# Reordering the first splits of a decoder layer, and placing two gate units between the memory's key units

## The chip, the cores and the metric

The kernel runs on one core of one Trainium2 chip. The metric is the device time of one execution in microseconds (us). Before the change it is 808.86 us, the median of three runs (808.32 to 809.01).

The engines are named as the profile does: PE is TensorE, whose sequence of matmuls is followed here, and PEld its weight loads; ACT is ScalarE, DVE VectorE, POOL GpSimd, and SP SyncE, which issues most transfers.

## The reference, cut to what matters

One layer of a decoder over 512 tokens of width 1024, in float32. The normalised input `u` is projected by one wide matrix, and its columns feed three branches: sliding-window attention, stick-breaking attention and cross-attention to a memory of 256 rows. Each branch's output is projected back, multiplied by the sigmoid of its own gate columns, and the three are added. An output projection and a gated feed-forward network follow.

```python
u = rms_norm(h, ln_mix_pre[l])
proj = jnp.einsum('bsd,de->bse', u, w_in[l])
qa, ka, va, qb, kb, vb, qm, gl = jnp.split(proj, split_idx, axis=-1)
y_swa = swa_sink_attention(qa, ka, va, swa_sinks[l], rel_bias)
y_sb = stick_breaking_attention(qb, kb, vb)
mkv = jnp.einsum('bmd,de->bme', rms_norm(mem, ln_mem[l]), w_mem_kv[l])
mk, mv = jnp.split(mkv, 2, axis=-1)
y_mem = memory_cross_attention(qm, mk, mv)
g = jax.nn.sigmoid(gl.reshape(B, S, N_BRANCH, D))
...
```

(The reshapes to heads are left out of the calls.)

## The kernel before, in words

**Numbers.** Every float32 operand of the large products is split into a high part of the fp32r type (a copy on ScalarE) and a low part (value minus high part, on VectorE); see `split`, L132 to L139. A product is then three matmuls, high by high, high by low and low by high (`mm3`, L164 to L168). In the profile a row `hi<-raw` is the first half of a split, `lo<-raw,hi` the second.

**The stream of weight units.** `Stream` (L33) holds a list of units: each has a weight block of 128 x 1024 numbers (512 KB), loaded through SP, split into hi and lo, and then used by a generator that issues matmuls. When a unit begins, loads up to four units ahead and splits up to three units ahead are put out (`ahead`, L58; constants L28 and L29). A unit's generator yields after each small group of matmuls the time that the group is taken to cost: 0.65 for three matmuls of 512 columns, 0.325 for three of 256. A projection or gate unit (`proj`, L278; `gate`, L306) has eight groups of 0.65; a unit of the memory's keys (`mem_keys`, L374) eight groups of 0.325; a unit of its values (`mem_vals`, L389) four groups of 0.65.

**Who asks for units.** The attention code runs beside the stream. `sb_head` (L620) does one head of the stick-breaking branch: a first group of score matmuls into three banks `z`, then on ScalarE and VectorE a chain (Abs, Exp, Ln, maximum, splits sh and sl), `yield 7.0`, a second group of matmuls into `z` (sums of the chain's results), three Exp on ScalarE, and `yield 3.0`. After every second head, a product with the values (`ysb`) follows. At each yield the loop at L802 lets the stream put out units worth that time (`dn.run`). So eight heads take 80 of the stream's time, and whatever units come next lie between the heads.

**Order on the engines.** The program's order is only a wish: a planner orders the instructions of each engine at build time, by program order where it holds an instruction for ready. At the start (`with tc.manual_schedule()`, L506 to L555) the order is as written.

**Banks.** The accumulators of projections, gates, keys and values come from a pool of two PSUM banks (`psd`, L110), those of heads from a pool of six (`psa`). A unit's bank is free again when VectorE has evacuated it: L290 for projections and gates, L383 for keys, L401 for values. A key unit uses one bank; the four value units together accumulate into both.

**The order of units** (L435 to L467): four `kb`, four `qb`, six units of values of the tokens, `ka`, `qa0`, `qa1`, four key units, four value units, `qa2`, `qa3`, the eight gates of the stick-breaking branch, and so on. The memory is loaded when `ka` is loaded (`mem_load`) and split when `qa1` is split (`mem_split`).

**The start.** Before the stream runs, the first three units (`kb0` to `kb2`) are loaded in three pieces: chunks 0 and 1 of the eight along the inner dimension (128 x 256 numbers), then 2 to 4, then 5 to 7 (`first_load`, L497; `PIECE`, L492). x is loaded transposed, in eight chunks of 128 x 512. `first_split` (L502) splits one unit's piece; `gain_split` (L485) multiplies one chunk of x by its gain and splits it (`gained`, L235: L237 on ScalarE gives `uh`, L238 on VectorE gives `ul`). TensorE begins with ten warm-up matmuls on an idle tile, then takes nine matmuls for chunk 0 of the three units in an order written out by hand (L543 to L546), and then, chunk by chunk, unit by unit (L547 to L550). Behind the third unit's last chunk comes the sum of squares `ss_x` from `xacc` (L534 to L538).

Of the kernel before, what the change touches and what calls it, by code (L numbers as in the profile page):

```python
# [17 lines left out]
P = 128  # L18
# [3 lines left out]
KC = D // P  # L22
# [4 lines left out]
SWA, SB, MEM = 0, 1, 2  # L27
# [76 lines left out]
def tile_kernel(ctx, tc, a):  # L104
# [13 lines left out]
    def ck(name, dt=F32):  # L118
        return ckp.tile([P, 512], dt, tag="ck", name=name)
# [42 lines left out]
    dn = Stream(w_load, w_split)  # L162

    def mm3(out, l, r, start, stop):  # L164
        (lh, ll), (rh, rl) = l, r
        nc.tensor.matmul(out, lh, rh, start=start, stop=False, skip_group_check=True)  # L166
        nc.tensor.matmul(out, lh, rl, start=False, stop=False, skip_group_check=True)  # L167
        nc.tensor.matmul(out, ll, rh, start=False, stop=stop, skip_group_check=True)  # L168

    def mm(out, l, r, start, stop):  # L170
        return nc.tensor.matmul(out, l, r, start=start, stop=stop, skip_group_check=True)  # L171

    def cols(hl, o, n):
        return hl[0][:, o : o + n], hl[1][:, o : o + n]
# [68 lines left out]
    u = [None] * KC  # L243

    def parts(name, t):
        h, l = ck(f"{name}h", F32R), ck(f"{name}l", F32R)
        split(t[:, :], h[:, :], l[:, :])
        return h, l

    def stack_parts(kind, idx, t):  # L250

        for e in range(2):
            r, o = 64 * e, 64 - 64 * e
            x = ck(f"{kind}s{idx}{e}", F32R)
            nc.scalar.copy(x[r : r + 64, :], t[r : r + 64, :])
            nc.vector.tensor_tensor(
                x[o : o + 64, :], t[r : r + 64, :], x[r : r + 64, :].bitcast(F32), op=ALU.subtract
            )
            st[(kind + "s", idx, e)] = x

    def stack_twice(kind, idx, t):

        for e in range(2):
            r, o = 64 * e, 64 - 64 * e
            x = ck(f"{kind}s{idx}{e}", F32R)
            lo = ck(f"{kind}l{idx}{e}", F32R)
            nc.gpsimd.memset(lo[o : o + 64, :].bitcast(F32), 0.0)
            st[(kind + "l", idx, e)] = lo
            nc.scalar.copy(x[r : r + 64, :], t[r : r + 64, :])
            nc.vector.tensor_tensor(  # L270
                lo[r : r + 64, :], t[r : r + 64, :], x[r : r + 64, :].bitcast(F32), op=ALU.subtract
            )
            nc.vector.tensor_copy(x[o : o + 64, :], t[r : r + 64, :])
            st[(kind + "s", idx, e)] = x

    first_ps = {}

    def proj(kind, idx):  # L278
        def gen(hi, lo):
            begun = first_ps.get((kind, idx))  # L280
            ps = begun or (aps if kind == "kb" or (kind, idx) == ("qb", 2) else dps)(f"{kind}{idx}")
            for k in range(1 if begun else 0, KC):
                mm3(ps[:, :], cols((hi, lo), k * P, P), u[k], k == 0, k == KC - 1)
                yield 0.65
            t = ck(f"{kind}{idx}")
            s = 0.125 if kind in ("qa", "qb") else 1.0

            def evac():
                with tc.high_priority():
                    nc.vector.scalar_tensor_tensor(t[:, :], ps[:, :], s, st["rb"][:, :], op0=ALU.mult, op1=ALU.mult)  # L290
                if kind in ("kb", "qa"):
                    stack_parts(kind, idx, t)
                elif kind in ("qb", "ka"):
                    stack_twice(kind, idx, t)
                elif kind == "qm":
                    st[("qms", idx)] = parts(f"qms{idx}", t)

            if "rb" in st:
                evac()
            else:  # L300
                st.setdefault("waiting", []).append(evac)
            st[(kind, idx)] = t

        return gen
# [69 lines left out]
    def mem_keys(i):  # L374
        def gen(hi, lo):
            if i % 2 == 0:
                st[("mk", i // 2)] = ck(f"mk{i}")
            t = st[("mk", i // 2)][:, (i % 2) * M : (i % 2 + 1) * M]
            ps = dps(f"pmk{i}")
            for k in range(KC):  # L380
                mm3(ps[:, :M], cols((hi, lo), k * P, P), mu[k], k == 0, k == KC - 1)
                yield 0.325
            nc.vector.tensor_tensor(t, ps[:, :M], st["mrb"][:, :], op=ALU.mult)  # L383
            if i % 2 == 1:
                st[("mks", i // 2)] = parts(f"mks{i // 2}", st[("mk", i // 2)])

        return gen
# [49 lines left out]
    for h in range(2):  # L437
        for q in range(3):
            n = 3 if q < 2 else 2
# [3 lines left out]
    def add_proj(kind, idx, ci):  # L443
        src = a["w_p"][:, ci].rearrange("p k n -> p (k n)")
        dn.add(src, 1024, gate(int(kind[1]), idx) if kind[0] == "g" else proj(kind, idx))
# [1 line left out]
    add_proj("ka", 0, 16)  # L447
    dn.on_load(mem_load)
    add_proj("qa", 0, 12)
    add_proj("qa", 1, 13)  # L450
    dn.on_split(mem_split)
    for i in range(4):
        dn.add(a["w_mk"][:, i].rearrange("p k n -> p (k n)"), 1024, mem_keys(i))
    for q in range(4):
        dn.add(a["w_mv"][:, 2 * q : 2 * q + 2].rearrange("p k n -> p (k n)"), 1024, mem_vals(q))
    add_proj("qa", 2, 14)
    add_proj("qa", 3, 15)
    for b, order in ((SB, 0), (SWA, 1), (MEM, 2)):
        for c in range(8):
            add_proj(f"g{b}", c, 17 + 3 * c + b)  # L460
        dn.mark(f"gates{b}")
        if b == SB:
            for i in range(4):
                add_proj("qm", i, 8 + i)
        for c2 in range(4):
            dn.add(a["w_br"][:, b, 2 * c2 : 2 * c2 + 2].rearrange("p c k n -> p (c k n)"), 1024, branch(b, c2, order))
        dn.mark(f"branch{b}")  # L467
# [17 lines left out]
    def gain_split(k):  # L485
        h, l = ck(f"uh{k}", F32R), ck(f"ul{k}", F32R)
        gained(xraw[k][:, :], g_pre[:, k : k + 1], h[:, :], l[:, :])
        u[k] = (h[:, :], l[:, :])


    FIRST = 3
    PIECE = ((0, 2), (2, 5), (5, 8))  # L492
    raws = [wp.tile([P, 1024], F32, tag="raw", name=f"raw_first{i}") for i in range(FIRST)]
    his = [wp.tile([P, 1024], F32R, tag="hi", name=f"hi_first{i}", bufs=4) for i in range(FIRST)]
    los = [wp.tile([P, 1024], F32R, tag="lo", name=f"lo_first{i}", bufs=4) for i in range(FIRST)]
# [6 lines left out]
    def first_split(i, p):  # L502
        sl = slice(PIECE[p][0] * P, PIECE[p][1] * P)
        split(raws[i][:, sl], his[i][:, sl], los[i][:, sl])

    with tc.manual_schedule():  # L506

        idle = cst.tile([P, 512], BF16, name="idle")
        nc.vector.memset(idle[:, :], 0.0)
        pw = dps("warm")  # L510
        for i in range(WARM):
            mm(pw[:, :], idle[:, :P], idle[:, :], True, True)

        first_load(nc.scalar, 0)
        first_table = nc.scalar.preload_act_table_set("natural_log_exp_and_others")
        load_x(0, 3)
        first_load(nc.sync, 1)
        load_x(3, 5)
        first_load(nc.sync, 2)
        load_x(5, 8)  # L520
        dn.loaded = dn.have = FIRST
        first_split(0, 0)
        gain_split(0)
        for i in range(1, FIRST):
            first_split(i, 0)
        gain_split(1)
        gain_split(2)
        for p in (1, 2):
            for i in range(FIRST):
                first_split(i, p)  # L530
            for k in range(*PIECE[p]):
                if u[k] is None:
                    gain_split(k)
        xacc = ck("xacc")  # L534
        nc.scalar.activation(xacc[:, :], xraw[0][:, :], AF.Square)
        for k in range(1, KC):
            nc.scalar.activation(xraw[k][:, :], xraw[k][:, :], AF.Square)
            nc.vector.tensor_tensor(xacc[:, :], xacc[:, :], xraw[k][:, :], op=ALU.add)  # L538
        dn.ahead(4, 3)

        for i in range(FIRST):
            first_ps[("kb", i)] = aps(f"kb{i}")
        for n, (i, w, r) in enumerate(  # L543
            ((0, his, 0), (0, los, 0), (1, his, 0), (0, his, 1), (1, his, 1), (1, los, 0), (2, his, 0), (2, his, 1), (2, los, 0))
        ):
            mm(first_ps[("kb", i)][:, :], w[i][:, :P], u[0][r], n in (0, 2, 6), False)  # L546
        gens = [dn.units[i]["mm"](his[i], los[i]) for i in range(FIRST)]  # L547
        for k in range(1, KC + 1):
            for g in gens:
                next(g, None)  # L550
        dn.at = FIRST
        st["rs"], st["rb"] = rstd_of("x", xacc, S, aps)
        st["chain"] = since[-1]
        for f in st.pop("waiting"):
            f()  # L555
# [864 lines left out]
```

## Time and profile before

| what | value |
|---|---|
| median of three runs | 808.86 us |
| lowest, highest | 808.32, 809.01 us |
| the profiled execution's own time | 808.77 us |
| its span, first to last instruction | 807.0 us |
| granted TensorE clock, mean | 0.998 |

Rows of the profile name the line, engine and operation, then `output<-inputs`, partitions and elements. In a timeline the first two numbers are the start and the duration in us, and brackets at the end give the idle time of the engine before that row and what ended it. In the list of waits the numbers are the sum, the count and the longest in us. The row of a stretch gives its length, the busy time and count of PE, PEld, DVE, ACT and POOL, the granted clock, the share of the DMA engines and GB/s. Matmul rows overlap one another, so that the distance between starts tells the pace and not the duration.

### The profile page before, as it was taken

To read this page: it belongs to the slowest core of one execution; us is meant where nothing else is said; L and a number is where in the kernel's file an instruction comes from. 1 tells how busy PE (TensorE), PEld (TensorE's weight loads), DVE (VectorE), ACT (ScalarE), POOL (GpSimd) and SP (SyncE) were. 2 spreads that over 40 slices of the span, in tenths; PEclk is the share of its full clock that TensorE was granted. 3 is DMA by queue.
4 is the path that set the end of the run, shared out by engine and by line. 5 is a ranking of instruction groups with operands and counts; after the bars stand their busy time and mean duration, and the time that the engine had idled before them with its cause. 6 is when DMAs were issued, how large, how long until landed. Compare 5 with 4: busy or idle time off the path is not lost.

```text
span 807.0 us, 12317 instructions
## 1 busy us (share of the span) xinstructions
PE 797.5 (99%) x4710; PEld 701.1 (87%) x4710; DVE 587.3 (73%) x937; ACT 439.7 (54%) x787; POOL 88.7 (11%) x108
## 2 busy tenths in 40 slices
PE   9999999999999999999999999999999999999996
PEld 6899897778788888888888899999999999988885
DVE  7895878556588833873394869877676777898797
ACT  7562776555655432552272567654444445666573
POOL 1203200000000000320004200010000000205200
PEclk9999999999999999999999999999999999999999
DMA  7444526112222223213359936977777662759902
GB/s 270 140 122 137 189 79 183 53 52 69 63 79 58 90 88 89 69 53 105 97 167 377 234 65 172 264 200 203 186 175 192 174 170 82 180 129 224 211 0 105
DMA packets 37692, 112.95 MB, mean 140 GB/s; under 512 B 4480, under 2 KB 6192, under 8 KB 37632
## 3 DMA queue, kind: packets, MB, share of 16 engines
q1 hardware_dynamic: 29184, 86.32, 33.5%
q0 software_dynamic: 8016, 25.44, 16.7%
q8 instruction: 37, 0.61, 0.3%
q10 hardware_dynamic: 432, 0.39, 0.1%
q14 instruction: 23, 0.19, 0.1%
HBM read 108.46 MB, written 3.67 MB: 139 GB/s over the span
## 4 chain that ended last, share of the span: by engine, by line
PE 96%; DVE 1%; ACT 1%; DMA 1%; issue 1%; ACTq 0%; DVEq 0%
PE g L166 5%; PE g L168 5%; PE g L167 5%; PE gx L166 5%; PE gx L168 5%; PE gx L167 5%; PE z L171 3%; PE br L166 3%; PE br L167 3%; PE br L168 3%; PE gy L168 3%; PE gy L166 3%; PE gy L167 3%; PE x L166 2%; PE x L168 2%; PE x L167 2%
## 5 line engine op out<-in xcount | busy, mean ns | idle before, releaser
L134 ACT CAST hi<-gw 128x1024 fp32r<-128x1024 f32 x77 | 79.7, 1048 | 82.6 <-DVE gw L1005 39.2
L134 ACT CAST hi<-raw 128x1024 fp32r<-128x1024 f32 (+2 forms) x64 | 65.8, 1035 | 101.3 <-issue 49.4
L135 DVE TENSOR_TENSOR lo<-gw,hi 128x1024 fp32r<-128x1024 f32 x77 | 93.4, 1222 | 32.4 <-ACT hi L134 32.4
L135 DVE TENSOR_TENSOR lo<-raw,hi 128x1024 fp32r<-128x1024 f32 (+2 forms) x64 | 78.0, 1219 | 14.8 <-ACT hi L134 14.7
L166 PE MATMUL g<-uh,hi 128*128 128x512 f32 x192 | 75.6, 394 | 0.0
L168 PE MATMUL g<-uh,lo 128*128 128x512 f32 x192 | 74.8, 389 | 0.0
L167 PE MATMUL g<-ul,hi 128*128 128x512 f32 x192 | 74.8, 389 | 0.0
L290 DVE SCALAR_TENSOR_TENSOR g<-g,rb_x 128x512 f32<-128x512 f32 x24 | 16.4, 689 | 54.6 <-PE g L168 54.5
L987 POOL DMA_DIRECT2D gw<-in_w_gu x27 | 23.4, 905 | 187.9 <-DMA gw<-in_w_gu 83.3
L166 PEld LDWEIGHTS g<-uh,hi 128*128 128x128 f32 x192 | 36.1, 188 | 8.1 <-issue 1.0
L168 PEld LDWEIGHTS g<-uh,lo 128*128 128x128 f32 x192 | 36.0, 188 | 7.6
L167 PEld LDWEIGHTS g<-ul,hi 128*128 128x128 f32 x192 | 36.1, 188 | 7.2
L167 PE MATMUL x<-lo,lh 128*128 128x512 f32 x88 | 34.3, 389 | 0.0
L166 PE MATMUL x<-hi,lh 128*128 128x512 f32 x88 | 34.3, 389 | 0.0
L134 ACT CAST hi<-r 128x1024 fp32r<-128x1024 f32 (+1 forms) x24 | 23.6, 982 | 19.6 <-PE y L168 5.3
L168 PE MATMUL x<-hi,ll 128*128 128x512 f32 x88 | 34.1, 389 | 0.0
L135 DVE TENSOR_TENSOR lo<-r,hi 128x1024 fp32r<-128x1024 f32 (+1 forms) x24 | 27.1, 1129 | 3.2 <-ACT hi L134 3.1
L184 ACT ACTIVATE e<-e 128x384 f32<-128x384 f32 (+1 forms) x48 | 26.9, 561 | 1.5
L135 DVE TENSOR_TENSOR lo<-bp,hi 128x512 fp32r<-128x512 f32 x33 | 22.8, 724 | 6.1 <-ACT hi L134 6.0
L134 ACT CAST hi<-bp 128x512 fp32r<-128x512 f32 x33 | 19.1, 620 | 13.6 <-PE y L168 4.8
L654 DVE SCALAR_TENSOR_TENSOR e<-z,e 128x384 f32<-128x384 f32 (+1 forms) x24 | 14.3, 596 | 15.7 <-ACT e L184 15.7
L166 PE MATMUL gx<-B11h,hi 128*128 128x256 f32 x88 | 25.1, 285 | 0.2 <-ACT B11h L916 0.2
(548 smaller groups left out, 2614.3 us busy)
## 6 DMA issues: line engine op xcount, KB each, us to landing
gw<-in_w_gu SPq DMA_DIRECT2D x57, 512.0 KB, 5.3
raw<-in_w_p SPq DMA_DIRECT2D x38, 512.0 KB, 3.6
gw<-in_w_gu POOLq DMA_DIRECT2D x27, 512.0 KB, 7.6
raw<-in_w_br SPq DMA_DIRECT2D x12, 512.0 KB, 3.8
bp<-in_w_dn SPq DMA_DIRECT2D x22, 256.0 KB, 8.2
r<-in_w_dn POOLq DMA_DIRECT2D x10, 512.0 KB, 8.5
raw<-in_w_out SPq DMA_DIRECT2D x8, 512.0 KB, 3.8
bp<-in_w_dn POOLq DMA_DIRECT2D x11, 256.0 KB, 13.2
```

Of the source, the lines that this page charges most:

```text
L134: ins = nc.scalar.copy(hi, raw)
L135: lows = nc.vector.tensor_tensor(lo, raw, hi.bitcast(F32), op=ALU.subtract)
L166: nc.tensor.matmul(out, lh, rh, start=start, stop=False, skip_group_check=True)
L167: nc.tensor.matmul(out, lh, rl, start=False, stop=False, skip_group_check=True)
L168: nc.tensor.matmul(out, ll, rh, start=False, stop=stop, skip_group_check=True)
L171: return nc.tensor.matmul(out, l, r, start=start, stop=stop, skip_group_check=True)
L184: ins = nc.scalar.activation(*args, **kw)
L290: nc.vector.scalar_tensor_tensor(t[:, :], ps[:, :], s, st["rb"][:, :], op0=ALU.mult, op1=ALU.mult)
L654: nc.vector.scalar_tensor_tensor(x, z[i][:, :n], 0.0, x, op0=ALU.max, op1=ALU.add)
L987: nc.gpsimd.dma_start(gw[(n, key)][:, :], g_src(n, i, j), accum_op=ALU.add)
```

## The change

At the start, a piece of a unit and a chunk of x alternate on ScalarE and VectorE: unit 0, chunk 0, unit 1, chunk 1, unit 2, chunk 2, where before it was unit 0, chunk 0, units 1 and 2, chunks 1 and 2. TensorE takes chunk 0 of units 0 and 1 in the order that it had, then chunk 1 of units 0 and 1, then chunks 0 and 1 of unit 2. The stream's generators of these three units go on with chunk 2.

In the stream, `qa1` moves behind the value units, beside `qa2` and `qa3`. Gate 0 of the stick-breaking branch comes between the second and third key units, and gate 1 between the fourth and the value units. The memory is split when the first key unit is split, which is the unit at the same place of the list as `qa1` was. The list stays as long as it was.

```diff
-            for k in range(1 if begun else 0, KC):
+            for k in range(2 if begun else 0, KC):
...
-    add_proj("qa", 1, 13)
-    dn.on_split(mem_split)
+
     for i in range(4):
         dn.add(a["w_mk"][:, i].rearrange("p k n -> p (k n)"), 1024, mem_keys(i))
+        if i == 0:
+            dn.on_split(mem_split)
+        if i % 2 == 1:
+            add_proj(f"g{SB}", i // 2, 17 + 3 * (i // 2) + SB)
     for q in range(4):
         dn.add(a["w_mv"][:, 2 * q : 2 * q + 2].rearrange("p k n -> p (k n)"), 1024, mem_vals(q))
-    add_proj("qa", 2, 14)
-    add_proj("qa", 3, 15)
+    for i in range(1, 4):
+        add_proj("qa", i, 12 + i)
     for b, order in ((SB, 0), (SWA, 1), (MEM, 2)):
-        for c in range(8):
+        for c in range(2 if b == SB else 0, 8):
...
-        first_split(0, 0)
-        gain_split(0)
-        for i in range(1, FIRST):
+        for i in range(FIRST):
             first_split(i, 0)
-        gain_split(1)
-        gain_split(2)
+            gain_split(i)
...
-        for n, (i, w, r) in enumerate(
-            ((0, his, 0), (0, los, 0), (1, his, 0), (0, his, 1), (1, his, 1), (1, los, 0), (2, his, 0), (2, his, 1), (2, los, 0))
-        ):
-            mm(first_ps[("kb", i)][:, :], w[i][:, :P], u[0][r], n in (0, 2, 6), False)
+        order = [(0, 0, "hh"), (0, 0, "lh"), (1, 0, "hh"), (0, 0, "hl"), (1, 0, "hl"), (1, 0, "lh")]
+        order += [(i, k, x) for i, k in ((0, 1), (1, 1), (2, 0), (2, 1)) for x in ("hh", "lh", "hl")]
+        for i, k, x in order:
+            w = (his if x[0] == "h" else los)[i]
+            mm(first_ps[("kb", i)][:, :], w[:, k * P : (k + 1) * P], u[k][x[1] == "l"], k == 0 and x == "hh", False)
         gens = [dn.units[i]["mm"](his[i], los[i]) for i in range(FIRST)]
-        for k in range(1, KC + 1):
+        for k in range(2, KC + 1):
```

## The prediction

> **What bounds the kernel now.** I read the page first, then what TensorE waited for, then the stretches, then the rows around each wait. From the page:
>
> ```profile
> PE 797.5 (99%) x4710; PEld 701.1 (87%) x4710; DVE 587.3 (73%) x937; ACT 439.7 (54%) x787; POOL 88.7 (11%) x108
> ```
>
> TensorE is busy 99% of the span. The change adds and removes no matmul, so it can give back only what TensorE loses between matmuls, and it can lose any amount. The view of the waits of TensorE lists what it lost to other engines. It has five rows; of these, two lie where the diff doesn't reach (the warm-up before any data, and a later stage), and three are in the two places that it edits:
>
> ```profile
> PE ysb L171 <- ACT e L184: 1.1, 1, 1.1
> PE kb L167 <- DVE ul L238: 0.2, 1, 0.2
> PE pmv L166 <- DVE mk L383: 0.2, 1, 0.2
> ```
>
> They are 1.5 us in sum. The stretch that holds two of them:
>
> ```profile
> 120.00:140.00 20.00, 18.71 (x97) 15.77 (x97) 17.12 (x25) 13.80 (x24) 0.00 (x0) 1.00 0.59 173
> ```
>
> TensorE was busy for 18.71 of 20.00 us: 1.29 idle, which are the ysb wait and the pmv wait. The granted clock was 1.00.
>
> **Part 1, the start.** The timeline of TensorE:
>
> ```profile
> 6.31 0.62 PE L171 MATMUL kb<-ul,hi_first 128*128 128x512 f32 x2
> 6.77 0.40 PE L171 MATMUL kb<-uh,lo_first 128*128 128x512 f32 x1
> ...
> 8.48 0.50 PE L167 MATMUL kb<-ul,hi_first 128*128 128x512 f32 x1 [0.22 <-DVE ul L238]
> 8.82 0.40 PE L168 MATMUL kb<-uh,lo_first 128*128 128x512 f32 x1
> 9.06 0.40 PE L166 MATMUL kb<-uh,hi_first 128*128 128x512 f32 x1
> ```
>
> Unhindered, one start follows another after 0.23 to 0.24 us (two from 6.31 to 6.77, one from 8.82 to 9.06). The rows at 6.77 and 8.82 are the sixth matmul of the list written out by hand and the third behind its nine: six steps, which need 6 x 0.235 = 1.41 and took 2.05. So **0.64 us** is lost, three times what the waits list names, because restarts after a wait count as busy. What was late, on ScalarE and then on VectorE:
>
> ```profile
> 5.12 0.41 ACT L134 CAST hi_first<-raw_first 128x256 fp32r<-128x256 f32 x1
> 6.60 0.41 ACT L134 CAST hi_first<-raw_first 128x256 fp32r<-128x256 f32 x1 [1.08 <-DMA raw_first<-in_w_p]
> 6.92 1.33 ACT L237 ACTIVATE uh<-xT,xg 128x512 fp32r<-128x512 f32 x2
> ```
>
> ```profile
> 5.88 0.42 DVE L135 TENSOR_TENSOR lo_first<-raw_first,hi_first 128x256 fp32r<-128x256 f32 x1
> ...
> 7.67 1.41 DVE L238 SCALAR_TENSOR_TENSOR ul<-xT,xg,uh 128x512 fp32r<-128x512 f32 x2 [0.20 <-ACT uh L237]
> ```
>
> ScalarE stands 1.08 us until the third unit's weights land, with chunk 1 of x queued behind them. The view of tile xT, for its first transfer alone:
>
> ```profile
> L482 SPq DMA_DIRECT2D xT<-in_xT x1: 421/421/421, 1.2 to 1.2; - x1
> ...
> DMA to landing us min/median/max: 3.7/3.7/3.7
> ```
>
> Chunk 1 is there at 1.2 + 3.7 = 4.9. With the new order its gain split (half of 1.33, 0.7) begins on ScalarE near 5.12 + 0.41 = 5.5, inside the idle time, and ends by 6.2. VectorE is free at 6.30 and has the low half by 7.05 (half of 1.41 is 0.7). The new order of matmuls asks for that chunk at 6.77 + 0.23 = 7.00 and for its low half two starts later, 7.47: both are there. The third unit's weights, cast from 6.60 to 7.01, are asked for after six more starts, near 8.4. So no wait is left, and I take the whole 0.64. The casts after it move up by one gain split, about 0.6, so they aren't later than now. Nothing is issued anew: the loads and their queues stay as they are. The next thing that could hold TensorE is the sum of squares:
>
> ```profile
> 19.47 1.49 DVE L538 TENSOR_TENSOR xacc<-xacc,xT 128x512 f32<-128x512 f32 x2
> ```
>
> It ends at 20.96. TensorE's row that needs it:
>
> ```profile
> 22.71 1.02 PE L171 MATMUL ss_x<-xacc,ones 128*128 128x512 f32 x2
> ```
>
> 22.71 - 0.64 = 22.07 is still 1.1 us later than 20.96, so the gain isn't given back there.
>
> The Trainium skill, "TensorE: Matmul & The Clock Gate", section "Back-to-back issue gap", gives a warm gap of N/2.4 + 2.5 ns, 216 ns at 512 columns. By it the six steps would need 1.30 and the gain would be 0.75 and the sum 806.9, an estimate; the rows show 0.23 to 0.24, and they decide.
>
> **Part 2, the memory stage.** No instruction is added; units trade places, each with its load and its split. The loads:
>
> ```profile
> raw<-in_w_p SPq DMA_DIRECT2D x38, 512.0 KB, 3.6
> ```
>
> They are asked for four units ahead and land in 3.6 us. By the costs in the code four key or value units last 4 x 2.6 = 10.4, and with gates between them longer, so I cost the loads at nothing; they would cost what a load is late if that cover went. The splits keep their number and, with a gate between the keys, get more time on ScalarE and VectorE. In the stream's own costs a projection or gate is 8 x 0.65 = 5.2, a key or value unit 2.6. Before, ka, qa0, qa1 (15.6), four key units and four value units (20.8) end at 36.4. Each head takes 7.0 and 3.0, so head 3's second group of score matmuls (z) is put out at 37, when the next unit is qa2. It needs a psd bank, and the value units hold both until they are evacuated (L401). The timelines of TensorE and ScalarE and the view of tile pmv:
>
> ```profile
> 134.65 0.39 PE L171 MATMUL z<-sh,ntri_r 128*128 128x512 f32 x1
> ...
> 136.63 0.38 PE L171 MATMUL z<-e,none 128*128 128x128 f32 x2
> 138.12 0.44 PE L171 MATMUL ysb<-e,v_all 128*64 128x128 f32 x4 [1.11 <-ACT e L184]
> 138.49 0.50 PE L166 MATMUL qa<-uh,hi 128*128 128x512 f32 x1
> ```
>
> ```profile
> 136.71 1.36 ACT L184 ACTIVATE e<-z 128x512 f32<-128x512 f32 x3 [0.81 <-PE z L171]
> ```
>
> ```profile
> L401 DVE TENSOR_SCALAR mv<-pmv,rs_m x2: 742/744/745, 135.3 to 139.2; 128x512 f32<-128x512 f32 x2
> ```
>
> So ysb stands ahead of qa2 on TensorE, which waits 1.11 us for three Exp. After the change the sum is 5.2 x 2 + 2.6 x 2 + 5.2 + 2.6 x 2 + 5.2 = 31.2 before the first value unit: at 37 the stream is in the third, with 41.6 - 37 = 4.6 of matmuls left whose banks are already theirs. The 3.0 between z and ysb can then stand where they stand in the program, and cover 1.36 of Exp. I take **1.11** away.
>
> The 0.18 wait of pmv I leave in the sum. Its rows, TensorE then VectorE:
>
> ```profile
> 123.67 0.47 PE L166 MATMUL pmv<-hi,mh 128*128 128x512 f32 x1 [0.18 <-DVE mk L383]
> ```
>
> ```profile
> 123.11 0.74 DVE L383 TENSOR_TENSOR mk<-pmk,rb_m 128x256 f32<-128x256 f32 x2
> ```
>
> The unit after the keys needs a bank that VectorE frees late. That unit becomes a gate, and the same wait can meet it: between 0.2 gained and the losses of the first rival below.
>
> The sum: 808.77 of the profiled execution (span 807.0 and 1.77 around it) - 0.64 - 1.11 = **807.0**. The median of before, 808.86, is 0.09 higher. A measurement tells about 0.2% from no change, 1.6 us: faster is below 807.2, slower above 810.5.
>
> **The rivals.** What speaks against part 2 is how late VectorE evacuates a long unit beside a head's chain. The timeline of TensorE, then VectorE:
>
> ```profile
> 96.43 0.39 PE L166 MATMUL qa<-uh,hi 128*128 128x512 f32 x1
> ...
> 101.87 0.39 PE L171 MATMUL z<-sh,ntri_r 128*128 128x512 f32 x1
> ...
> 104.19 0.28 PE L167 MATMUL pmk<-ml,hi 128*128 128x256 f32 x1
> 104.31 0.28 PE L168 MATMUL pmk<-mh,lo 128*128 128x256 f32 x1
> ```
>
> ```profile
> 101.96 0.68 DVE L290 SCALAR_TENSOR_TENSOR qa<-qa,rb_x 128x512 f32<-128x512 f32 x1
> ```
>
> At 96.43 qa1 follows on qa0, which is evacuated at 101.96, 5.53 later. Now qa1 covers that with 101.87 - 96.43 = 5.44; after the change the first key unit stands there, 24 x 0.12 = 2.88.
>
> - **Slower**: the evacuation stays behind the chain, and the short units don't cover it. The second key unit needs qa0's bank: 5.44 - 2.88 = 2.56 short. The second value bank needs that of the second gate, with three matmuls (0.68) ahead: 5.53 - 0.68 = 4.85 short, less the z group (134.65 to 136.63 + 0.38, 2.36) that can stand in between, 2.5. Together 5.05: 812.1. It decides once 3.5 of the 5.05 is real. For it: these rows. Against it: at 101.87 the z group stands between qa1 and the keys, so the planner fills with z where a unit isn't ready, and head 2's first group could stand there too. Chance 0.18. The Trainium skill, "Perfetto Trace Analysis", section "Matmuls", has independent groups rotate through PSUM banks so that an evacuation overlaps the next group. By it two banks do and the sum stays 807.0; the rows show that this held only with a next group as long as the lag.
> - **One of the two places**: the 2.56 at the key unit alone, 809.6, within 0.2%. Chance 0.10.
> - **The wait stays**: the planner again puts ysb ahead of the stream, or another unit's bank is late by as much. Only the start gains: 808.77 - 0.64 = 808.1. Chance 0.17.
> - **The start doesn't do what it says**: chunk 1 lands after the third unit's weights, and ScalarE still stands. 808.77 - 1.11 = 807.7. Against it is the landing at 4.9. Chance 0.05.
> - **All goes**: the pmv wait and its restart too, about 0.5 more, 806.5. Chance 0.08.
>
> **How the numbers follow.** The forecast has 0.42, with a range of its own of 806.6 to 807.6 for restarts that I didn't count; 0.34 of it lies below 807.2. Faster: 0.34 + 0.08 = 0.42. Slower: 0.18. Within 0.2%: 0.08 + 0.17 + 0.05 + 0.10 = 0.40. The range leaves out the slower rival and little at the low end, and reaches past 809.6: 806.2 to 810.2.
>
> **What would show it.** Part 1 is right if ScalarE has no 1.08 us gap before the third cast and TensorE's start at the first chunk-2 matmul is some 0.6 earlier; wrong if a gap remains between 6.7 and 9. Part 2 is right if the ysb wait for Exp is off the list of waits and no wait for VectorE (L290, L383) by a pmk or pmv matmul takes its place; the slower rival shows as just those, 2.5 us each. If the time is off and these rows are as said, the loss is downstream, where I claim that nothing moves.

## The result, and the profile after

The changed kernel takes 815.88 us, the median of six runs (815.39 to 816.16); the kernel before, run beside it, 808.8 (808.32 to 809.01). The ratio is 1.0088, with a 95% interval of 1.0075 to 1.0101: 7.1 us slower, where 1.8 us faster was forecast. The profiled execution has a span of 813.9 us, 6.9 more than before.

The first part of the page of after, the busy time of each engine:

```profile
PE 801.1 (98%) x4710; PEld 702.5 (86%) x4710; DVE 588.4 (72%) x937; ACT 440.2 (54%) x787; POOL 88.5 (11%) x108
```

TensorE has the same 4710 matmuls and its busy time rose by 3.6 us, though no work was added; the rest of the 6.9 is idle. So part of the loss is matmuls that take longer, and restarts after a wait, which count as busy. The waits of TensorE, after (sum, count, longest):

```profile
PE z L171 <- DVE sl L661: 3.4, 4, 1.1
PE z L171 <- DVE sh L660: 1.4, 3, 0.6
```

The three waits that the prediction set out from (ysb, kb, pmv) are gone. In their place stand seven new ones, of a head's second group of score matmuls (`z`) for the chain's results (`sh`, `sl`) on VectorE. Two stretches of after hold five of the seven (length, then busy time and count of PE, PEld, DVE, ACT, POOL, granted clock, DMA share, GB/s):

```profile
150.00:155.00 5.00, 3.42 (x16) 1.86 (x15) 4.79 (x10) 3.60 (x7) 0.00 (x0) 1.00 0.01 2
155.00:160.00 5.00, 3.95 (x14) 3.20 (x13) 3.19 (x6) 2.50 (x5) 0.00 (x0) 0.68 0.36 105
```

TensorE starts 30 matmul rows in 10 us there, VectorE is busy for 4.79 of the first 5.00, and the granted clock falls to 0.68. This is head 4. The timeline of TensorE in after:

```profile
148.78 0.39 PE L168 MATMUL pmv<-hi,ml 128*128 128x512 f32 x1
149.01 0.40 PE L171 MATMUL z<-qbs,kbs 128*128 128x512 f32 x1
...
150.30 0.40 PE L171 MATMUL z<-negmb,identb 128*128 128x128 bf16 x3
151.05 0.51 PE L171 MATMUL z<-sh,ntri_r 128*128 128x512 f32 x1 [0.36 <-DVE sh L660]
...
156.22 0.44 PE L171 MATMUL z<-sl,ntri_r 128*128 128x384 f32 x1 [1.05 <-DVE sl L661]
...
156.98 0.78 PE L166 MATMUL qa<-uh,hi 128*128 128x512 f32 x1
157.55 0.63 PE L167 MATMUL qa<-ul,hi 128*128 128x512 f32 x1
...
160.11 0.43 PE L167 MATMUL qa<-ul,hi 128*128 128x512 f32 x1
160.38 0.39 PE L168 MATMUL qa<-uh,lo 128*128 128x512 f32 x1
```

The last matmul of the values starts at 148.78. The next unit of the stream, `qa1`, starts at 156.98. In between TensorE has only score matmuls: the first group of the next head, put forward to 149.01, and then head 4's second group, which can go no faster than its chain. The timeline of VectorE at the same place:

```profile
149.84 0.69 DVE L655 SCALAR_TENSOR_TENSOR e<-z,e 128x512 f32<-128x512 f32 x1 [2.19 <-ACT e L184]
...
154.35 1.22 DVE L135 TENSOR_TENSOR lo<-raw,hi 128x1024 fp32r<-128x1024 f32 x1
155.48 0.69 DVE L661 TENSOR_TENSOR sl<-e,sh 128x512 fp32r<-128x512 f32 x1
156.08 0.75 DVE L401 TENSOR_SCALAR mv<-pmv,rs_m 128x512 f32<-128x512 f32 x1
...
158.56 0.74 DVE L401 TENSOR_SCALAR mv<-pmv,rs_m 128x512 f32<-128x512 f32 x1
```

The values hold both banks of the pool of two until L401 has read them, at 156.08 and 158.56, behind the whole chain (149.84 to 156.17). VectorE had even stood idle for 2.19 us before the chain, within which the values ended (148.78 + 0.39 = 149.17); but in the order that the planner gave it, the evacuation stands behind the chain.

What head 4 costs: the three small matmuls at 150.30 need some 0.15 (in before three such start at 122.46, and the next matmul at 122.61), so the second group could start at 150.45; unhindered it takes 2.36 (the prediction's figure). 156.98 - 150.45 - 2.36 = 4.2 us of stall. Behind it, from 156.98 to 160.11, seven steps took 3.13 where seven of 0.23 take 1.61: 1.5 us more. Together 5.7.

The other two waits of 1.06 us are heads 1 and 2. TensorE in after, then VectorE:

```profile
100.34 0.39 PE L171 MATMUL z<-sh,none_r 128*128 128x256 f32 x2
101.79 0.45 PE L171 MATMUL z<-sl,ntri_r 128*128 128x384 f32 x1 [1.06 <-DVE sl L661]
...
102.49 0.36 PE L166 MATMUL pmk<-mh,hi 128*128 128x256 f32 x1
...
122.74 0.44 PE L171 MATMUL z<-sl,ntri_r 128*128 128x384 f32 x1 [1.06 <-DVE sl L661]
```

```profile
99.92 1.22 DVE L135 TENSOR_TENSOR lo<-raw,hi 128x1024 fp32r<-128x1024 f32 x1
101.05 0.69 DVE L661 TENSOR_TENSOR sl<-e,sh 128x512 fp32r<-128x512 f32 x1
101.65 0.69 DVE L290 SCALAR_TENSOR_TENSOR qa<-qa,rb_x 128x512 f32<-128x512 f32 x1
```

The second key unit starts at 102.49; it needs the bank of `qa0`, which VectorE frees from 101.65 on, behind the chain. So the second z group stands ahead of it, and that group waits for the last `sl`. In the middle of the chain stands the low half of a weight split, 1.22 us long (99.92). The step from 100.34 to 101.79 is 1.45 and would be two of 0.12: 1.2 lost. Head 2 is the same with gate 0's bank: 1.2 again.

At the start, ScalarE in after:

```profile
5.29 0.41 ACT L134 CAST hi_first<-raw_first 128x256 fp32r<-128x256 f32 x1
5.60 0.72 ACT L237 ACTIVATE uh<-xT,xg 128x512 fp32r<-128x512 f32 x1
6.45 0.41 ACT L134 CAST hi_first<-raw_first 128x256 fp32r<-128x256 f32 x1
```

Chunk 1's gain split fills the time in which ScalarE had waited, and the third cast has no wait. TensorE's first matmuls on data, and the sum of squares:

```profile
5.38 0.85 PE L171 MATMUL kb<-uh,hi_first 128*128 128x512 f32 x1
6.02 0.63 PE L171 MATMUL kb<-uh,lo_first 128*128 128x512 f32 x1
6.45 0.47 PE L171 MATMUL kb<-uh,hi_first 128*128 128x512 f32 x1
...
7.22 0.39 PE L171 MATMUL kb<-uh,lo_first 128*128 128x512 f32 x1
...
22.41 1.02 PE L171 MATMUL ss_x<-xacc,ones 128*128 128x512 f32 x2
```

The sum of squares came 0.30 us earlier than before, not 0.64.

### The profile page after: what moved, and what is told of

Its sections match the earlier page's. It is cut to its first block, busy times and chain, and to the rows that moved or that the text cites. A ratio compares the mean times of both kernels' runs of the same rounds, so it can differ in the third digit from the quotient of the medians.

```text
span 813.9 us, 12317 instructions
## 1 busy us (share of the span) xinstructions
PE 801.1 (98%) x4710; PEld 702.5 (86%) x4710; DVE 588.4 (72%) x937; ACT 440.2 (54%) x787; POOL 88.5 (11%) x108
## 4 chain that ended last, share of the span: by engine, by line
PE 95%; DVE 3%; issue 1%; ACT 1%; DVEq 0%; ACTq 0%
PE g L166 5%; PE g L168 5%; PE g L167 5%; PE gx L166 5%; PE gx L168 5%; PE gx L167 5%; PE br L166 3%; PE br L168 3%; PE br L167 3%; PE gy L168 3%; PE gy L166 3%; PE gy L167 3%; PE x L167 2%; PE x L166 2%; PE x L168 2%; PE z L171 2%
```

## The experiments

**The theory** (A): `qa1` behind the values finds no bank, because their evacuations stand behind the chain of a head whose first group was just put out; while the stream stands, TensorE can only follow that chain. **The rivals**: (B) the start shifts everything so that chains and units meet badly; (C) the gates between the keys do the harm, as long units with late evacuations; (D) the loss is not the bank but something else at that place: a late load or split, or the place in the head where the values end.

**One part at a time.** e1 has the three hunks of the start alone, e2 the rest of the diff alone.

> The start edits alone, with the units in the order of before. Theory A (the loss is in the memory stage: TensorE waits while the banks that the next unit needs stand behind a head's chain on VectorE): 0.3 to 0.65 us faster than before, 808.2 to 808.5, with the ysb wait of 1.1 us as before. Rival B (the start edits bring part of the loss): slower than before.

Measured: 807.98 us (807.71 to 808.87), ratio 0.9994 (0.9984 to 1.0003) against 808.74. The waits of TensorE in e1 still have the line of before:

```profile
PE ysb L171 <- ACT e L184: 1.1, 1, 1.1
```

That is 0.2 below the range expected, and the interval reaches over 1: the start neither causes the loss nor gains more than can be told from no change.

> The new order of units alone, with the start of before. Theory A: all of the loss and a bit more, 816.0 to 816.5, with the waits of z for sl and sh as in the changed kernel and the ysb wait gone. Rival B: clearly less than the 7 us, below 814.

Measured: 816.04 us (815.64 to 816.83), ratio 1.0091 (1.0076 to 1.0106). With the old start the list of waits has the same sums and counts for z, 3.4 (4) and 1.4 (3). All of the loss is in the order of the units; B falls.

**Which of the two moves.** e3 puts `qa1` back ahead of the keys and keeps the gates between them:

```diff
     add_proj("qa", 0, 12)
+    add_proj("qa", 1, 13)
+    dn.on_split(mem_split)
...
-    for i in range(1, 4):
+    for i in range(2, 4):
         add_proj("qa", i, 12 + i)
```

> The changed kernel, but qa1 stays ahead of the key units; the two gate units stand between them as in the change. The values then end at 46.8 of the stream's time, just ahead of head 4's second group (47), not just behind its first (41.6). Theory A (what costs is where the values end against a head, and the short unit beside qa0): no wait of 5 us, 807.5 to 809.5. Rival C (gates between the keys cost in themselves): 811 or more.

Measured: 807.59 us (807.22 to 808.14), ratio 0.9986 (0.9977 to 0.9995). The waits of TensorE in e3 have one line at this place:

```profile
PE qa L166 <- ACT e L184: 0.7, 1, 0.7
```

e4 does the reverse: `qa1` behind the values, no gate between the keys.

```diff
-        if i % 2 == 1:
-            add_proj(f"g{SB}", i // 2, 17 + 3 * (i // 2) + SB)
...
-        for c in range(2 if b == SB else 0, 8):
+        for c in range(8):
```

> The changed kernel without gates between the keys; qa1 only moves behind the values. The values then end at 31.2, just behind head 3's first group (30). Theory A: TensorE waits for head 3's chain with almost no matmuls to cover it, 5 to 7 us, and 1.2 us at head 1: 813 to 817. Rival C (it is the gates that cost): 808 to 810.

Measured: 816.56 us (816.26 to 817.33), ratio 1.0098 (1.0082 to 1.0113). The waits of TensorE in e4, and two stretches:

```profile
PE z L171 <- DVE sh L658: 2.5, 2, 2.3
PE z L171 <- DVE sl L659: 1.7, 2, 1.1
```

```profile
130.00:135.00 5.00, 2.60 (x6) 1.41 (x6) 3.59 (x7) 4.84 (x9) 0.00 (x0) 0.75 0.32 102
135.00:140.00 5.00, 4.18 (x14) 3.18 (x13) 3.47 (x7) 1.57 (x5) 0.00 (x0) 0.50 0.34 103
```

C falls as a cause of its own: the gates alone cost nothing (0.9986 of before), and the move of `qa1` alone costs as much as the whole change. (With `qa1` moved, gate 0's late evacuation is still what stands behind head 2's wait of 1.06 in after, as said above; e4 has no such wait.) The stall lies now at head 3. In the stream's costs the values end at 15.6 - 5.2 + 20.8 = 31.2, which is 1.2 behind head 3's first group at 30; in after they end 1.6 behind head 4's at 40; in e3 at 46.8, when head 4's chain is nearly through. The stall goes where the values end just behind a head's first group.

**The place of the values' end.** e5 is after, with head 3 giving the stream 1.6 more, so that the values end ahead of head 4's first group:

```diff
-        yield 3.0
+        yield 4.6 if h == 3 else 3.0
```

> The changed kernel with one number changed: the last yield of head 3 is 4.6 for 3.0, so that the value units end ahead of head 4's first group and not behind it. No unit moves. Theory A (qa1 can't start because the value banks are evacuated behind head 4's chain): the 5 us of waits near 150 us go, 810.3 to 811.3. Rival D (the loss is that of the order of units as such, or a load that is late): 815 or more.

Measured: 809.46 us (809.18 to 810.09), ratio 1.001 (1.0001 to 1.002), 0.8 below the range expected. The term for the clock had been left out of it; with it, 815.88 - 5.7 = 810.2 is still 0.7 too high. The waits of TensorE, and the stretch of the stall, in e5:

```profile
PE z L171 <- DVE sl L661: 2.1, 2, 1.1
```

```profile
155.00:160.00 5.00, 5.00 (x32) 4.58 (x31) 4.89 (x8) 2.72 (x5) 0.00 (x0) 1.00 0.37 105
```

In the two profiled executions the span is 813.9 - 808.1 = 5.8 shorter, near the 5.7 worked out above; the medians differ by 6.4, since the execution of e5 that was profiled lies 0.4 above its median and that of after 0.2 below. The clock is 1.00. Heads 1 and 2 still wait, 2.1.

**The low half in the chain.** e6 is after, with the low halves of the weights ordered behind the last `sl` of the chain:

```diff
-            nc.vector.tensor_tensor(sl[i][:, :n], x, sh[i][:, :n].bitcast(F32), op=ALU.subtract)
+            st["sums"] = nc.vector.tensor_tensor(sl[i][:, :n], x, sh[i][:, :n].bitcast(F32), op=ALU.subtract)
...
+        if "chain" in st and "sums" in st:
+            after(lows, st["sums"])
```

> The changed kernel, in which no low half of a weight split may stand ahead of the last low half of a head's chain on VectorE (it stands between its last two operations now). Theory A (each z wait of 1.05 us is that split of 1.22): 1.2 us less at heads 1, 2 and 4, 812.2 to 813.5. Rival E (the chain itself is late, and the split only stands in a gap): under 1 us less, 814.9 or more.

Measured: 812.8 us (810.92 to 813.13), ratio 1.0047 (1.0033 to 1.0061), within the range of theory A; E falls. VectorE at head 4 in e6:

```profile
148.29 0.69 DVE L657 SCALAR_TENSOR_TENSOR e<-z,e 128x512 f32<-128x512 f32 x1 [2.19 <-ACT e L186]
...
152.91 0.69 DVE L663 TENSOR_TENSOR sl<-e,sh 128x512 fp32r<-128x512 f32 x1
153.52 0.75 DVE L403 TENSOR_SCALAR mv<-pmv,rs_m 128x512 f32<-128x512 f32 x1
```

From the chain's first row to the evacuation it is 5.23 now, where it was 6.24. The waits of 1.06 at heads 1 and 2 are gone; the stall of head 4 is shorter and stays: from the start of the last matmul of the values to that of `qa1` it is 7.30 us (147.46 to 154.76), where it was 8.20.

**Both.** e7 has the edits of e5 and e6 together.

> Both edits of the last two together. If the two causes are separate and are all of the loss: 807.0 to 808.5, and no wait of z for sl or sh above 0.3 us. If more is behind it: above 809.5.

Measured: 808.51 us (807.93 to 808.81), ratio 0.9996 (0.9987 to 1.0005), 0.01 above the range expected. No wait for `sh` or `sl` is left in the list. Shorter ones, which the list leaves out, remain at heads 1 and 2. TensorE at head 1 in e7:

```profile
99.57 0.33 PE L173 MATMUL z<-sl,none_r 128*128 128x384 f32 x1
100.03 0.44 PE L173 MATMUL z<-sh,ntri_r 128*128 128x384 f32 x1
100.32 0.39 PE L173 MATMUL z<-sh,none_r 128*128 128x256 f32 x2
100.83 0.45 PE L173 MATMUL z<-sl,ntri_r 128*128 128x384 f32 x1
```

Call the median distance between two starts, for matmuls of one shape, their pace: 0.227 us at 512 columns, 0.174 at 384, 0.120 at 256. The first step here is 0.46 where the pace is 0.17, the third 0.51 where two of 0.12 make 0.24. Added up over heads 1 and 2 (96 to 131), TensorE lies 1.4 us further behind its pace in e7 than in before; from 131 to 140, where the ysb wait was, it lies 1.7 less behind. So the new order has no loss on balance, and no gain that can be told either.

**The bank itself.** e5 moved the end of the values; D could still say that the place does it and not the bank. e9 is after, and only `qa1`'s bank comes from the pool of six:

```diff
-            ps = begun or (aps if kind == "kb" or (kind, idx) == ("qb", 2) else dps)(f"{kind}{idx}")
+            ps = begun or (aps if kind == "kb" or (kind, idx) in (("qb", 2), ("qa", 1)) else dps)(f"{kind}{idx}")
```

> The changed kernel in which qa1 takes its PSUM bank from the pool of six instead of the pool of two; the order of the units, the heads' chains and the evacuations of the values are untouched. If the loss near 150 is that qa1 finds no bank because the values' evacuations stand behind head 4's chain, qa1 follows directly on the values, the stall of 150.3 to 157 goes with the clock's drop behind it, and the two waits of 1.1 us for sl at heads 1 and 2 stay: about 809.5 (808.8 to 810.3). If it is lost because units behind the values are late for another reason (load, split) or because of where the values end in the head, nothing changes: 815.4 to 816.4.

Measured: 810.56 us (810.2 to 811.18), ratio 1.0024 (1.0015 to 1.0033). TensorE in e9, then VectorE:

```profile
148.59 0.39 PE L168 MATMUL pmv<-hi,ml 128*128 128x512 f32 x1
148.81 0.40 PE L166 MATMUL qa<-uh,hi 128*128 128x512 f32 x1
...
171.44 0.44 PE L171 MATMUL z<-sl,ntri_r 128*128 128x384 f32 x1 [0.68 <-DVE sl L661]
```

```profile
155.89 0.74 DVE L401 TENSOR_SCALAR mv<-pmv,rs_m 128x512 f32<-128x512 f32 x1
...
159.06 0.74 DVE L401 TENSOR_SCALAR mv<-pmv,rs_m 128x512 f32<-128x512 f32 x1
```

The evacuations are as late as in after, the values end at the same place of the head, and yet `qa1` follows on the values at once. So it is the bank, and not a late load or split, nor the place of the values' end: D falls. The time is 0.3 above the range expected, for a reason that none of the theories had: a third wait for `sl`, at 171.44, where VectorE again has a low half in the chain and TensorE lost 0.8.

> The kernel of the bank for qa1 and, besides, the low halves of the weights ordered behind the last sl of a chain. If the two mechanisms are all that the change loses, both stalls go: 807.8 to 808.8, near the 808.51 of the kernel with the later values and the low halves behind the chain. If another loss hides behind them it stays over 809.5.

e10 has the edits of e9 and e6 together. Measured: 808.13 us (807.93 to 808.89), ratio 0.9995 (0.9987 to 1.0004) against 808.68, within the range expected. The list has no wait for `sh` or `sl` any more, that of 171.44 included.

**A better kernel.** e8 is e3 with the low halves behind the chain.

> The kernel with qa1 ahead of the keys and gates between them (807.6), with the low halves behind the chain as well. Theory A: what is left there, a wait of 0.7 us of qa for an Exp, doesn't hang on the split; 806.9 to 807.6. Rival E: the splits come later, and the units behind them; slower than 807.8.

Measured: 806.95 us (806.72 to 807.71), ratio 0.9981 (0.9972 to 0.999) against 808.73, below before and after, and within the range expected. All the waits of TensorE that its list still has:

```profile
PE warm L173 <- DVE idle L514: 1.4, 1, 1.4
PE gx L168 <- ACT B11h L919: 0.2, 1, 0.2
```

## Why the prediction was wrong, by its own steps

**Part 1 was right in its mechanism, but took the loss of one execution for a fixed one.** The split of chunk 1 went into ScalarE's idle time. TensorE's sixth matmul on data, the same in both orders, starts at 6.77 in before and at 7.22 in after, and `ss_x` at 22.71 and 22.41: 15.94 and 15.19 us, 0.75 less, near the 0.64. But the sixth matmul came 0.45 later in after: the first started 0.14 later (5.38 for 5.24), and the five steps from it took 1.84 for 1.53, one of them 0.43 (6.02 to 6.45). So the sign that was named, some 0.6 earlier, came as 0.30. Nor does the old order always lose the 0.64: in e2, which has it, the third unit's cast began at 6.30 and not at 6.60, and the stretch from the sixth matmul to `ss_x` is 15.25 (7.14 to 22.39), as short as in e1 with the new order, 15.22 (6.57 to 21.79). The medians give 0.8 (e1 against before) and 0.2 (after against e2).

**Part 2 was right in what it removes.** The ysb wait is off the list, as forecast: ScalarE's three Exp are covered by value matmuls. The pmv wait, which the forecast had left in, is gone too. The ysb term was larger than the 1.11 of the list: with the restart behind the wait, TensorE lies 1.7 us less behind its pace there.

**The step that failed** is that part 2 ends its sum at head 3: "at 37 the stream is in the third, with 41.6 - 37 = 4.6 of matmuls left whose banks are already theirs". That is true, but I stopped at 37 and so put all that comes behind it at nothing. The same sum says that the values end at 41.6, 1.6 behind head 4's first group at 40. I didn't ask what comes next, `qa1`, nor whose bank it needs. It needs one that VectorE frees only behind head 4's chain, and that cost 5.7 us (e9 against after: 4.9 of span and 0.8 of the new wait). "The slower rival" had this mechanism, an evacuation behind the chain, but at two other places. Its 2.56 at the second key unit was 1.2, since the z group stood in between as I had argued against it; its 2.5 at the second value bank did not occur; head 2, not named, cost 1.2; and the costliest place was outside my list. Its chance was 0.18, and even its 812.1 lay below what came.

**The sum, with what was measured**, as time that TensorE lies behind its pace, after less before: -0.3 (start), +2.9 (heads 1 and 2, from 96 to 131: the two waits of 1.2, and shorter ones and restarts beside them, less the pmv wait), -1.7 (ysb, from 131 to 140), +0.2 (restarts from 140 to 149), +4.3 (the stall of head 4), +1.5 (the clock behind it) = +6.9, the difference of the spans.

**The claim at the end of the prediction**, "the loss is downstream, where I claim that nothing moves", named the right place to look. What was wrong was to claim it without going through the heads one by one.

## What to carry to other kernels

When units change places in a stream that other work cuts into, add up the stream's time anew for every cut, and for each ask which unit starts there, whose bank it needs and where that bank's evacuation stands in its engine's order. A bank pool of two holds only while the unit in flight lasts longer than the evacuation lags (here up to 7 us behind a chain, against key units of 2.9); a unit that holds both banks should end ahead of a long chain on the evacuating engine, or the next unit should have a bank elsewhere. Work that isn't urgent, such as a split for a later unit, shouldn't stand within the chain that TensorE waits for.

## What the runs showed of the hardware that I had not expected

**The clock falls after a broken stretch.** In after no wait of TensorE between 150 and 157 is longer than 1.05 us, and it was busy for 3.42 of 5.00 us; yet the granted clock in the next 5 us is 0.68, and the matmuls of `qa1` start 0.43 us apart instead of 0.23 until 160.11. In e4, behind a wait of 2.33 us, the clock is 0.75 and 0.50 in the two stretches shown. So the stall cost a third more: 1.5 on top of 4.2. The Trainium skill, "TensorE: Matmul & The Clock Gate", section "Part 1: The HAM clock gate (the "warmup" mystery)", has the clock halved after an idle window of about 3.4 us; no single gap here was so long. Its section "A second HAM failure mode: psum-queue depth-cycling" tells of short idle times between groups of matmuls that also make it fall, which agrees. How much idle time in which window is enough, these runs don't show. In e6 one of the four runs took 810.92 us with a mean granted clock of 0.999, where the other three took 812.52 to 813.13 with 0.996 to 0.997; it has no trace, so that the clock stayed up behind its stall is likely and not shown.

**The first transfers land at varying times.** The third unit's cast on ScalarE begins, right behind a wait for its transfer, at 6.44 in e3, 6.62 in e1, 6.79 in e9 and 7.28 in e5, with the same code; in after it had landed by 6.45. In e5 ScalarE waited 1.08 us for it, as long as in the kernel before, and yet TensorE took 15.19 us from its sixth matmul to `ss_x` (7.22 to 22.41), as in after: the new order hides that wait. The pace at the very start varies as well. The step from the second to the third matmul on data is 0.23 us in before, e1 and e3, and 0.41 to 0.43 in after, e2 and e5, though the view of stretches gives a granted clock of 1.00 from 5 to 7 us in all six. One execution therefore can't tell a gain of half a microsecond at the start.
